# Keeping the split query weights of an expert layer in DRAM for the second choice of experts, with a sixth buffer for gathered rows

## The chip, the core and the metric

The kernel runs on one core of one Trainium2 chip. A core has five engines that run side by side and meet only at semaphores: PE (TensorE, the matmuls; PEld is its weight load), DVE (VectorE), ACT (ScalarE), POOL (GpSimd, which also issues the gathers) and SP (SyncE, which here only issues transfers). Each engine works through its own instructions in order. Sixteen DMA engines move data between DRAM and the on-chip memory. The metric is the device time of one execution in microseconds.

## What is computed

One encoder layer on 1024 tokens of width 1024: a norm, a combined projection, attention beside a retention branch, an output projection, and then a product-key expert layer on `xn = rmsnorm(x)`, which takes most of the time:

```
def peer_ffn(xn, w_query, sub_keys, expert_down, expert_up):
    def one_block(xb):                                  # 128 tokens
        q = (xb @ w_query).reshape(tb, 8, 2, 128)       # 8 heads, 2 halves
        s = einsum('thpd,hpnd->thpn', q, sub_keys)      # 128 keys each
        top_s, top_i = lax.top_k(s, 16)
        cand_s = top_s[:, :, 0, :, None] + top_s[:, :, 1, None, :]
        cand_i = top_i[:, :, 0, :, None] * 128 + top_i[:, :, 1, None, :]
        best_s, pos = lax.top_k(cand_s, 16)             # 128 experts a token
        eid = take_along_axis(cand_i, pos)
        gate = softmax(best_s)
        u = expert_down[eid]; act = gelu(einsum('thkd,td->thk', u, xb))
        v = expert_up[eid];   return einsum('thk,thkd->td', gate * act, v)
```

## The kernel before

**Two ways through the experts.** Tokens stand in tiles of 128. Five tiles (set B) pass through all 16384 experts as dense matmuls, with a gate matrix that is zero where an expert was not chosen. Three tiles (set A) gather only the chosen rows, one row per token and transfer. Both ways run at the same time in the last 1900 us: PE does the dense part, POOL issues gathers, and DVE consumes the gathered rows.

**Float32 by parts.** A matmul operand `w` is split into `wh`, a rounded copy (F32R), and `wl = w - wh`, and `mm3` (lines 72 to 75) makes a product of three matmuls. Each split costs a copy on ACT and a subtraction on DVE or POOL.

**The choice of experts** (`experts`, line 706) goes through 16 half heads `hp`. For each, `query` makes the projected query from the tokens and the weights of that half head (24 matmuls for two tiles), ACT and DVE split it, six matmuls per two tiles make the scores, and DVE picks the top 16 (`top16`) and combines the halves of a head (`choose`). It runs twice. The **early choice** (line 866) serves the five tiles of B and the first tile of A, has the weights in three buffers (`wb` = 3) and stands between the attention and the gate matrix. The **late choice** (line 962, inside `later`) serves the other two tiles of A. It is a generator of which `gathers` (line 1013) takes a step about once for each of the 128 groups of experts, so it lies inside the dense part. It has one weight buffer (`wb` = 1). In both, `weights` (line 642) loads `wqr`, 128 x 1152 floats or 576 KB, by SP, copies it to `wqh` on ACT and subtracts `wql` on POOL:

```
        def weights(pool, hp):
            wr = pool.tile([P, 9, P], F32, name="wqr")
            nc.sync.dma_start(wr, ap["wq"][hp])
            ...
            S.activation(wh, wr, AF.Copy)
            G.tensor_tensor(wl, wr, wh.bitcast(F32), op=ALU.subtract)
```

In the late choice the weights of `hp + 1` are asked for right after the scores of `hp` are issued, and the query of `hp + 1` is one step of the generator later.

**The dense part** goes through groups `a` of 128 experts. `down(a)` makes `pa` (48 matmuls on PE, lines 73 to 75), `up` makes `po` (30 matmuls per group, in five accumulators). After every second group DVE adds the five `po` to `acc` (line 1094), and the first `po` matmul of the next round waits for that addition. Per group SP loads `ur` (line 1034), `vr` twice (1079) and the gate `gt` (1043); ACT and DVE split them.

**The gathers** (`gather_tiles`, line 969): `rows` issues one indirect transfer of 512 KB on POOL into a buffer of the ring `rows` (line 977, `ROWS` = 5 buffers); a DVE instruction (line 988 for `peer_u`, 997 for `peer_v`) consumes it and frees the buffer. Six gathers belong to one group of the dense part. After the late choice a second ring of six (`rows2`) takes every second gather.

A scheduler puts the instructions of the engines in order from the program; the pools decide which tile may share room.

Of the kernel before, what the change touches and what calls it, by code (L numbers as in the profile page):

```python
# [10 lines left out]
F32 = mybir.dt.float32  # L11
F32R = mybir.dt.float32r
# [9 lines left out]
P = 128  # L22
# [6 lines left out]
HP = 16  # L29
# [6 lines left out]
RATE = 6.0  # L36
EVERY = 6
EARLY = 1.03
ROWS = 5

FIRST = 5
BEFORE = (10, 34, 58, 82, 106)
# [12 lines left out]
def peer_layer(tc, ap, dbg=None):  # L55
    nc = tc.nc
    V, S, G, PE = nc.vector, nc.scalar, nc.gpsimd, nc.tensor
# [14 lines left out]
    def mm3(out, ah, al, bh, bl, first, last):  # L72
        PE.matmul(out, ah, bh, start=first, stop=False)  # L73
        PE.matmul(out, ah, bl, start=False, stop=False)  # L74
        PE.matmul(out, al, bh, start=False, stop=last)  # L75

    with ExitStack() as top:
        const = top.enter_context(tc.tile_pool(name="const", bufs=1))
        dram = top.enter_context(tc.tile_pool(name="dram", bufs=1, space=DRAM))
# [41 lines left out]
        with ExitStack() as es:  # L121
# [212 lines left out]
            for gi, (half, nm) in enumerate(order):  # L334
# [4 lines left out]
                for c2 in range(DC // 2):  # L339
# [4 lines left out]
                    wh = pw.tile([P, 2, 512], F32R, name="wh", bufs=4)  # L344
                    wl = pw.tile([P, 2, 512], F32R, name="wl", bufs=4)
# [267 lines left out]
        w = (nB + 1) // 2 * P  # L613
# [4 lines left out]
        def query(pool, ps, segs, wh, wl, tag, aside):  # L618
            n = sum(e - b for seg in segs for _, b, e in seg)
            qh = pool.tile([P, n], F32R, name="pqh")  # L620
            ql = pool.tile([P, n], F32R, name="pql")
            at = 0
            for seg in segs:
                w = sum(e - b for _, b, e in seg)
                pq = ps.tile([P, w], F32, name=tag[0], bufs=tag[1])
                o = 0
                for nm, b, e in seg:
                    for c in range(DC):
                        mm3(pq[:, o:o + e - b], wh[:, c], wl[:, c], nT[nm][0][:, c, b:e], nT[nm][1][:, c, b:e],
                            c == 0, c == DC - 1)  # L630
                    o += e - b
                if aside:
                    q = pool.tile([P, w], F32, name="pqr")
                    S.activation(q, pq, AF.Copy)
                    split_q.append(S.activation(qh[:, at:at + w], pq, AF.Copy).ins)
                    G.tensor_tensor(ql[:, at:at + w], q, qh[:, at:at + w].bitcast(F32), op=ALU.subtract)
                else:
                    split(qh[:, at:at + w], ql[:, at:at + w], pq)
                at += w
            return qh, ql  # L640

        def weights(pool, hp):
            wr = pool.tile([P, 9, P], F32, name="wqr")
            nc.sync.dma_start(wr, ap["wq"][hp])
            wh = pool.tile([P, 9, P], F32R, name="wqh")
            wl = pool.tile([P, 9, P], F32R, name="wql")
            S.activation(wh, wr, AF.Copy)
            G.tensor_tensor(wl, wr, wh.bitcast(F32), op=ALU.subtract)
            return wh, wl

        pw0 = p0.enter_context(tc.tile_pool(name="wq0", bufs=1, side="right"))
        with ExitStack() as es:
# [26 lines left out]
            for u, (nm, i, t) in enumerate(todo):  # L679
# [4 lines left out]
                if u == 1:  # L684
                    first = weights(pw0, 0)
                if last is not None:
                    turned(ps, *last, "otp")
                    if last[0] == "A0":
                        first = first, query(pn, ps, SEGS, *first, ("pq", 1), False)
# [16 lines left out]
        def experts(sel, n, segs, pq_, pw, ps, wb, tags, bufs, first=None):  # L706
# [5 lines left out]
            def top16(vals, idxs, s, n, nm):  # L712
                V.max(vals[:, 0:8], s)
                V.max_index(idxs[:, 0:8], vals[:, 0:8], s)
                s2 = pw.tile([P, n], F32, name="s2" + nm)
                V.match_replace(s2, vals[:, 0:8], s, -3.4e38)
                V.max(vals[:, 8:16], s2)
                return V.max_index(idxs[:, 8:16], vals[:, 8:16], s2).ins
# [64 lines left out]
            def q_of(w):  # L783
                return query(pw, ps, segs, *w, (tags[0], bufs[0]), wb > 1)

            ws = {hp: weights(pq_[hp % wb], hp) for hp in range(first is not None, wb)}
            if first is not None:
                ws[0], cur = first
            else:
# [2 lines left out]
            for hp in range(HP):  # L792
                if hp % 2 == 0:
                    tv = pw.tile([P, n, 2, TOPK], F32, name="tv")
                    ti = pw.tile([P, n, 2, TOPK], U32, name="ti")
                (qh, ql), (wh, wl) = cur, ws[hp]
                more = hp + 1 < HP
                if wb > 1 and more and hp > 1:
                    cur = q_of(ws[hp + 1])
                yield  # L800
                sc = ps.tile([P, n, P], F32, name=tags[1], bufs=bufs[1])
                for t in range(n):
                    s = slice(t * P, t * P + P)
                    mm3(sc[:, t], qh[:, s], ql[:, s], wh[:, 8], wl[:, 8], True, True)
                if wb > 1 and more and hp < 2:
                    cur = q_of(ws[hp + 1])
                if hp + wb < HP:
                    ws[hp + wb] = weights(pq_[hp % wb], hp + wb)
                for t in range(n):
                    top = top16(tv[:, t, hp % 2], ti[:, t, hp % 2], sc[:, t], P, "s")  # L810
                    if t == 0:
                        first_top = top
                if hp % 2:
                    if wb > 1:
                        with tc.issue_after(first_top):
                            for _ in summing:
                                pass
                    else:
                        for _ in summing:
                            pass  # L820
                    waiting = hp // 2, pairs(tv), ti
                elif waiting:
                    summing = choose(*waiting)
                    next(summing)
                    waiting = None
                if wb == 1 and more:
                    yield
                    cur = q_of(ws[hp + 1])
# [33 lines left out]
        with ExitStack() as es:  # L862
            pq_ = {k: es.enter_context(tc.tile_pool(name=f"swq{k}", bufs=1)) for k in (1, 2, 0)}
# [84 lines left out]
        def later(ps):  # L948

            rest = SETS["A"][1:]  # L950
            with tc.tile_pool(name="se", bufs=1, side="right") as pe:
                n = len(rest)
                if n:
                    nT["A"] = [pe.tile([P, DC, n * P], F32R, name=n_) for n_ in ("nThA", "nTlA")]
                    for i, t in enumerate(rest):
                        xn = gp.tile([P, D], F32, name="rows", bufs=ROWS)
                        nc.sync.dma_start(xn, xn_dr[t])
# [11 lines left out]
        def gather_tiles(other):  # L969
            count = [0]  # L970

            def rows(table, idx):
# [3 lines left out]
                else:  # L976
                    u = gp.tile([P, D], F32, name="rows", bufs=ROWS)
                G.indirect_dma_start(out=u, out_offset=None, in_=table,  # L978
# [24 lines left out]
        with ExitStack() as es:  # L1003
# [108 lines left out]
            with tc.tile_pool(name="pro", bufs=1, side="right") as pp:  # L1112
                first = [pp.tile([P, DC * P], F32, name=f"first{a}") for a in range(FIRST)]
# [95 lines left out]
```

## Time and profile before

| What | us |
| --- | --- |
| median of three runs | 3129.86 (3127.61 to 3130.92) |
| the profiled execution, its own time | 3130.9 |
| its span, first to last instruction | 3129.1 |
| early choice, about | 630 to 890 |
| gate matrix, about | 890 to 1165 |
| dense part with the late choice in it, about | 1230 to 1930 |
| dense part without it, about | 1930 to 3087 |

The times of stages count from the span's start. Of the span PE is busy 91%, DVE 83%, POOL 55%, ACT 34%. These shares are means over stages with different limits, so the reading goes by stages.

### The profile page before, as it was taken

What the parts mean: (1) busy time and instruction counts of PE and PEld (TensorE: products, weight loads), DVE (VectorE), ACT (ScalarE), POOL (GpSimd) and SP (SyncE); (2) the same over time, 40 slices, a digit from 0 to 9 for tenths busy, and PEclk for the clock granted to TensorE, in tenths of its full rate; (3) what the DMA queues carried; (4) which work ended last, traced back from release to release, by engine and by line L of the source; (5) the groups of instructions that cost most, each with busy time, mean ns of one, the idle gap of its engine ahead of it and who ended that gap; (6) DMA issues with size and microseconds to landing.
All of it is one profiled execution on the core that took longest, in us unless ns stands there. A gap on an engine that the chain in (4) does not pass through costs nothing.

```text
span 3129.1 us, 44717 instructions
## 1 busy us (share of the span) xinstructions
PE 2850.7 (91%) x15999; PEld 2528.5 (81%) x15999; DVE 2589.1 (83%) x4867; ACT 1071.8 (34%) x1750; POOL 1706.6 (55%) x1319
## 2 busy tenths in 40 slices
PE   8999798898978847998899898999999999999998
PEld 6888577798977637887788787898999889998997
DVE  5465587579999946898998888888999988889997
ACT  4444466422247732222223222222222222222222
POOL 3422455346559944666556556565555465655551
PEclk9999899999999978999899999999999999999999
DMA  4334955331006688877777879999999899999994
GB/s 160 110 122 134 197 115 108 123 127 37 23 18 172 176 254 308 304 275 260 280 267 249 279 273 352 330 325 325 341 328 326 298 348 326 328 331 337 330 325 169
DMA packets 327919, 742.54 MB, mean 237 GB/s; under 512 B 25872, under 2 KB 133008, under 8 KB 327696
## 3 DMA queue, kind: packets, MB, share of 16 engines
q0 software_dynamic: 123520, 419.48, 39.2%
q1 hardware_dynamic: 201584, 315.28, 30.7%
q10 hardware_dynamic: 2592, 4.93, 0.5%
q8 instruction: 126, 2.06, 0.3%
q14 instruction: 97, 0.79, 0.1%
HBM read 669.26 MB, written 70.32 MB: 236 GB/s over the span
## 4 chain that ended last, share of the span: by engine, by line
PE 27%; DVE 15%; issue 14%; POOL 8%; DMA 5%; ACT 1%; SPq 1%; POOLq 0%; DVEq 0%; ACTq 0%
POOL rows L978 6%; PE po L73 5%; PE po L75 5%; PE po L74 5%; PE pa L73 4%; PE pa L74 4%; PE pa L75 4%; DVE gacc L997 4%; DVE rows L988 2%; DVE oh L910 2%; DMA rows<-peer_u,idx 2%; DMA ur<-ut 1%; POOL ao L917 1%; DVE acc L1094 1%; SPq L930 1%
## 5 line engine op out<-in xcount | busy, mean ns | idle before, releaser
L978 POOL DMA_INDIRECT rows<-peer_u,idx x384 | 525.8, 1369 | 401.6 <-DVE act L988 236.7
L978 POOL DMA_INDIRECT rows<-peer_v,idx x384 | 470.1, 1224 | 401.7 <-DVE gacc L997 338.4
L73 PE MATMUL pa<-nThB,uh 128*128 128x320 f32 x2048 | 639.0, 312 | 54.4 <-ACT uh L1050 39.4
L75 PE MATMUL pa<-nThB,ul 128*128 128x320 f32 x2048 | 636.0, 311 | 15.3 <-DVE ul L1051 15.3
L74 PE MATMUL pa<-nTlB,uh 128*128 128x320 f32 x2048 | 636.5, 311 | 0.0
L73 PE MATMUL po<-vh,hh 128*128 128x512 f32 x1280 | 516.0, 404 | 66.1 <-DVE acc L1094 65.9
L75 PE MATMUL po<-vh,hl 128*128 128x512 f32 x1280 | 509.6, 398 | 0.0
L74 PE MATMUL po<-vl,hh 128*128 128x512 f32 x1280 | 508.3, 397 | 0.7 <-DVE vl L1083 0.7
L997 DVE SCALAR_TENSOR_TENSOR gacc<-rows,act,gacc 128x1024 f32<-128x1024 f32 x384 | 502.9, 1310 | 5.5 <-DMA rows<-peer_v,idx 4.6
L988 DVE CUSTOM_DVE_ANT_0 rows<-rows,xng 128x1024 f32<-128x1024 f32 x384 | 467.0, 1246 | 44.8 <-DMA rows<-peer_u,idx 30.1
L73 PEld LDWEIGHTS pa<-nThB,uh 128*128 128x128 f32 x2048 | 389.9, 190 | 61.0 <-ACT uh L1050 39.6
L75 PEld LDWEIGHTS pa<-nThB,ul 128*128 128x128 f32 x2048 | 389.7, 190 | 16.6 <-DVE ul L1051 16.0
L74 PEld LDWEIGHTS pa<-nTlB,uh 128*128 128x128 f32 x2048 | 390.0, 190 | 4.4
L73 PEld LDWEIGHTS po<-vh,hh 128*128 128x128 f32 x1280 | 246.8, 193 | 124.5 <-DVE acc L1094 75.1
L1082 ACT ACTIVATE vh<-vr 128x512 fp32r<-128x512 f32 x256 | 160.2, 628 | 384.4 <-PE po L75 168.0
L75 PEld LDWEIGHTS po<-vh,hl 128*128 128x128 f32 x1280 | 246.2, 192 | 55.6
L74 PEld LDWEIGHTS po<-vl,hh 128*128 128x128 f32 x1280 | 246.7, 193 | 49.1 <-DVE vl L1083 1.5
L1050 ACT ACTIVATE uh<-ur 128x1024 fp32r<-128x1024 f32 x118 | 125.2, 1061 | 371.1 <-PE pa L74 199.1
L1051 DVE TENSOR_TENSOR ul<-ur,uh 128x1024 fp32r<-128x1024 f32 x118 | 145.7, 1234 | 102.6 <-ACT uh L1050 67.5
L917 POOL TENSOR_TENSOR ao<-oh,gT 128x512 f32<-128x512 bf16 x145 | 206.9, 1462 | 22.3 <-DVE oh L910 22.3
L923 PE MATMUL pg<-ao,bo 128*128 128x128 f32 x1280 | 181.5, 289 | 41.0 <-POOL ao L917 32.3
L858 ACT ACTIVATE hf<-pa 128x320 f32<-128x320 f32 x246 | 105.7, 430 | 328.4 <-PE pa L75 300.3
(344 smaller groups left out, 5481.3 us busy)
## 6 DMA issues: line engine op xcount, KB each, us to landing
vr<-peer_v SPq DMA_DIRECT2D x256, 256.0 KB
ur<-ut SPq DMA_DIRECT2D x123, 512.0 KB
g_dr<-stg SPq DMA_DIRECT2D x40, 1024.0 KB
gt<-g_dr SPq DMA_DIRECT2D x123, 320.0 KB
wr<-w_in SPq DMA_DIRECT2D x48, 512.0 KB
wqr<-wq SPq DMA_DIRECT2D x32, 576.0 KB
kt<-dk_dr POOLq DMA_DIRECT2D x16, 512.0 KB
xr<-xT SPq DMA_DIRECT2D x24, 256.0 KB
```

The lines of the kernel that those rows point to most:

```text
L73: PE.matmul(out, ah, bh, start=first, stop=False)
L74: PE.matmul(out, ah, bl, start=False, stop=False)
L75: PE.matmul(out, al, bh, start=False, stop=last)
L858: S.activation(hf[:, cs], pa, AF.Gelu)
L917: G.tensor_tensor(ao, oh[0], bc(gT[:, q:q + 4, None], [P, 4, P]), op=ALU.mult)
L923: PE.matmul(pg[:, j], bo[:, j], ao[:, j], start=True, stop=True)
L978: G.indirect_dma_start(out=u, out_offset=None, in_=table, in_offset=bass.IndirectOffsetOnAxis(ap=idx, axis=0))
L988: V.tensor_tensor_reduce(out=u, in0=u, in1=xn, scale=1.0, scalar=0.0, op0=ALU.mult, op1=ALU.add, accum_out=act[:, k:k + 1])
L997: V.scalar_tensor_tensor(o, v, act[:, k:k + 1], o, op0=ALU.mult, op1=ALU.add)
L1050: S.activation(uh, ur, AF.Copy)
L1051: V.tensor_tensor(ul, ur, uh.bitcast(F32), op=ALU.subtract)
L1082: S.activation(vh, vr, AF.Copy)
```

## The change

`weights` writes both parts of what it has split to a new DRAM tensor `wq_dr`, two stores of 576 KB on SP for each half head. The early choice goes through all 16 half heads, so all of them are written there (half head 0 by the call in the projection stage, line 685). The late choice calls `weights` with `made` true: no load of the raw weights, no copy on ACT, no subtraction on POOL; instead two loads of 576 KB, issued by POOL, straight into `wqh` and `wql`. Without `wqr` the late choice's pool is 4608 bytes a partition smaller, and `ROWS` goes from 5 to 6, which takes 4096.

```
-ROWS = 5
+ROWS = 6
...
-        def weights(pool, hp):
+
+        wq_dr = dram.tile([HP, 2, P, 9, P], F32, name="wq_dr")
+
+        def weights(pool, hp, made=False):
+            if made:
+                wp = [pool.tile([P, 9, P], F32R, name=n_) for n_ in ("wqh", "wql")]
+                for k in range(2):
+                    G.dma_start(wp[k], wq_dr[hp, k])
+                return wp
             wr = pool.tile([P, 9, P], F32, name="wqr")
             nc.sync.dma_start(wr, ap["wq"][hp])
...
             G.tensor_tensor(wl, wr, wh.bitcast(F32), op=ALU.subtract)
+            for k, w in enumerate((wh, wl)):
+                nc.sync.dma_start(wq_dr[hp, k], w.bitcast(F32))
             return wh, wl
...
-            ws = {hp: weights(pq_[hp % wb], hp) for hp in range(first is not None, wb)}
+            ws = {hp: weights(pq_[hp % wb], hp, wb == 1) for hp in range(first is not None, wb)}
...
-                    ws[hp + wb] = weights(pq_[hp % wb], hp + wb)
+                    ws[hp + wb] = weights(pq_[hp % wb], hp + wb, wb == 1)
```

Lines behind `weights` stand ten lines lower in the changed kernel (978 becomes 988, for instance).

POOL in the late choice, where it gathers rows of `peer_v`; before:

```order
L648 TENSOR_TENSOR wql<-wqr,wqh 128x1152
L978 DMA rows<-peer_v,idx 128x1024 x12
L648 TENSOR_TENSOR wql<-wqr,wqh 128x1152
L978 DMA rows<-peer_v,idx 128x1024 x13
L648 TENSOR_TENSOR wql<-wqr,wqh 128x1152
```

and now, at the same place:

```order
L649 DMA wqh<-wq_dr 128x1152
L649 DMA wql<-wq_dr 128x1152
L988 DMA rows<-peer_v,idx 128x1024 x13
L649 DMA wqh<-wq_dr 128x1152
L649 DMA wql<-wq_dr 128x1152
L988 DMA rows<-peer_v,idx 128x1024 x13
L649 DMA wqh<-wq_dr 128x1152
L649 DMA wql<-wq_dr 128x1152
```

Each subtraction has given its place between the gathers to two issues of transfers.

SP at the start of the late choice, where it loads for the dense part; before:

```order
L1034 DMA ur<-ut 128x1024
L1079 DMA vr<-peer_v 128x512
L644 DMA wqr<-wq 128x1152
L1034 DMA ur<-ut 128x1024
L1079 DMA vr<-peer_v 128x512 x2
L644 DMA wqr<-wq 128x1152
L1034 DMA ur<-ut 128x1024
```

and now:

```order
L1044 DMA ur<-ut 128x1024
L1089 DMA vr<-peer_v 128x512
L1044 DMA ur<-ut 128x1024
L1089 DMA vr<-peer_v 128x512 x2
L1044 DMA ur<-ut 128x1024
```

The loads of raw weights are gone from between those of the dense part.

SP in the middle of the early choice; before, six loads of raw weights in a row:

```order
L846 DMA ur<-ut 128x1024 x2
L644 DMA wqr<-wq 128x1152 x6
L879 DMA hf_dr<-hf 128x640
```

and now, of the same stretch, its beginning:

```order
L856 DMA ur<-ut 128x1024 x2
L658 DMA wq_dr<-wqh 128x1152
L658 DMA wq_dr<-wql 128x1152
L652 DMA wqr<-wq 128x1152
L658 DMA wq_dr<-wqh 128x1152
L658 DMA wq_dr<-wql 128x1152
L652 DMA wqr<-wq 128x1152
```

Two stores stand ahead of each load of raw weights.

## Rows read from the trace of the kernel before

**Rows 1.** Busy time by stage; columns: stretch, length, engines' busy us, clock, DMA share, GB/s.

```profile
630.00:890.00 260.00, 235.03 (x1657) 230.31 (x1655) 234.37 (x1308) 60.46 (x105) 145.73 (x95) 0.95 0.16 56
1230.00:1930.00 700.00, 630.12 (x3522) 569.60 (x3520) 625.83 (x1232) 194.86 (x298) 412.81 (x308) 0.95 0.80 277
1930.00:3087.00 1157.00, 1142.74 (x6328) 1035.17 (x6329) 1036.09 (x1380) 306.48 (x493) 644.27 (x498) 0.99 0.92 327
```

**Rows 2.** Waits, 1230 to 1930, PE's; columns: total us, times, longest us.

```profile
PE po L73 <- DVE acc L1094: 46.5, 16, 8.7
PE e L73 <- DVE cs L728: 7.1, 1, 7.1
PE e L73 <- DVE pql L67: 6.2, 1, 6.2
```

**Rows 3.** Waits, 1930 to 3087, PE's.

```profile
PE po L73 <- DVE acc L1094: 19.2, 10, 6.4
```

**Rows 4.** Timeline around one subtraction: start us, us, engine, line, names, [idle before].

```profile
1608.36 1.28 DVE L997 SCALAR_TENSOR_TENSOR gacc<-rows,act,gacc 128x1024 f32<-128x1024 f32 x1
...
1608.95 0.28 PE L75 MATMUL e<-wqh,pql 128*128 128x128 f32 x1
...
1610.86 3.09 POOL L648 TENSOR_TENSOR wql<-wqr,wqh 128x1152 fp32r<-128x1152 f32 x1
...
1611.55 3.48 DVE L997 SCALAR_TENSOR_TENSOR gacc<-rows,act,gacc 128x1024 f32<-128x1024 f32 x1
...
1618.34 0.67 DVE L1094 TENSOR_TENSOR acc<-po,acc 128x512 f32<-128x512 f32 x1
...
1619.06 0.50 PE L73 MATMUL po<-vh,hh 128*128 128x512 f32 x1 [2.05 <-DVE acc L1094]
```

**Rows 5.** Groups by line, 1230 to 1930: count, busy us, mean ns, idle before.

```profile
L997 DVE SCALAR_TENSOR_TENSOR gacc<-rows,act,gacc 128x1024 f32<-128x1024 f32 x128 | 175.6, 1372 | 4.9 <-DMA rows<-peer_v,idx 4.6
L988 DVE CUSTOM_DVE_ANT_0 rows<-rows,xng 128x1024 f32<-128x1024 f32 x115 | 147.8, 1306 | 21.4 <-DMA rows<-peer_u,idx 20.7 <-issue 0.6
...
L648 POOL TENSOR_TENSOR wql<-wqr,wqh 128x1152 fp32r<-128x1152 f32 x16 | 46.8, 2925 | 22.6 <-ACT wqh L647 22.2 <-issue 0.3
```

**Rows 6.** The same view, 1930 to 3087.

```profile
L997 DVE SCALAR_TENSOR_TENSOR gacc<-rows,act,gacc 128x1024 f32<-128x1024 f32 x251 | 320.9, 1279 | 0.7
L988 DVE CUSTOM_DVE_ANT_0 rows<-rows,xng 128x1024 f32<-128x1024 f32 x250 | 296.3, 1219 | 3.9 <-DMA rows<-peer_u,idx 3.9
```

**Rows 7.** Busy time, as rows 1, in two short stretches behind waits of PE.

```profile
1618.90:1623.00 4.10, 3.93 (x16) 2.92 (x17) 4.10 (x9) 1.07 (x2) 0.53 (x1) 1.00 0.72 259
1465.40:1469.00 3.60, 3.52 (x9) 2.79 (x10) 3.02 (x6) 0.10 (x1) 1.17 (x2) 0.55 0.93 311
```

**Rows 8.** Timeline of PE, the wait ahead of the second of these stretches.

```profile
1465.48 0.79 PE L73 MATMUL po<-vh,hh 128*128 128x512 f32 x1 [8.70 <-DVE acc L1094]
```

**Rows 9.** Waits, 1230 to 1930, DVE's.

```profile
DVE rows L988 <- DMA rows<-peer_u,idx: 20.7, 10, 5.3
DVE ul L1051 <- ACT uh L1050: 18.2, 7, 4.3
```

**Rows 10.** Waits of SP's queue, 1230 to 1930.

```profile
SPq L644 <- POOL wql L648: 72.1, 15, 11.7
```

**Rows 11.** Plain loads that POOL issues, in the attention: ns shortest/median/longest.

```profile
L111 POOL DMA_DIRECT2D kt<-dk_dr x16: 600/630/860, 313.1 to 482.7; - x16
```

**Rows 12.** Timeline, one gather and the DVE instruction that waits for it.

```profile
1855.21 0.98 POOL L978 DMA_INDIRECT rows<-peer_v,idx  x1 [4.94 <-DVE acc L1094]
...
1862.03 1.28 DVE L997 SCALAR_TENSOR_TENSOR gacc<-rows,act,gacc 128x1024 f32<-128x1024 f32 x1 [4.63 <-DMA rows<-peer_v,idx]
```

**Rows 13.** Timeline of PE, first matmuls of two queries.

```profile
1625.65 0.28 PE L73 MATMUL e<-nThA,wqh 128*128 128x256 f32 x1
...
1650.77 0.36 PE L73 MATMUL e<-nThA,wqh 128*128 128x256 f32 x1 [0.50 <-DVE eq L762]
```

**Rows 14.** Timeline of PE, last score matmul ahead of the second of them.

```profile
1642.91 0.28 PE L75 MATMUL e<-wqh,pql 128*128 128x128 f32 x1
```

**Rows 15.** Waits, 1230 to 1930, POOL's longest before a gather.

```profile
POOL rows L978 <- DVE gacc L997: 104.2, 68, 6.9
```

**Rows 16.** Waits in the early choice, 630 to 890, of PE and of SP's queue.

```profile
PE pq L75 <- POOL wql L648: 11.6, 4, 4.8
...
SPq L644 <- POOL wql L648: 87.6, 11, 20.0
```

## The prediction, made before the changed kernel ran

> **What bounds the kernel now.** I read the stages first, then who waits in the one that the change touches, then single instructions there. The table of stages [rows 1] sets two long stretches of the same dense work side by side. From 1930 to 3087 PE is busy 1142.74 of 1157 us at a mean granted clock of 0.99: PE is the bound. From 1230 to 1930, where the late choice runs in it, PE is busy 630.12 of 700 us at a mean clock of 0.95: it stands idle for 70 us and loses some 5% of 700, 35 us, to stretches at the lower of its two levels (1.2 instead of 2.4 GHz). So this stretch has at most about 105 us to give, and the other one its idle 14.
>
> Who makes PE wait there? DVE, nearly always: 46.5 us in 16 waits for the addition of line 1094, and two single waits of 7.1 and 6.2 for other DVE work [rows 2]. In the longer stretch without the late choice the same wait is 19.2 us [rows 3]. DVE is busy 625.83 of 700 us, 0.894, and its share is 0.896 from 1930 to 3087 and 0.901 in the early choice [rows 1]. So the late choice is bound by DVE as it really runs, with its short waits, and PE is let go late.
>
> The timeline shows why DVE is late [rows 4]. The instruction of line 997 takes 1.28 us at 1608.36. At 1610.86 POOL begins the subtraction `wql`, 3.09 us long; the same DVE instruction, begun at 1611.55 beside it, takes 3.48 us, 2.20 more. The addition for PE, behind it in DVE's order, starts only at 1618.34, and PE has stood for 2.05 us when it goes on at 1619.06. One subtraction has cost PE nearly what it cost DVE.
>
> **What the change removes in the late choice.** The 16 subtractions, 46.8 us of POOL with a mean of 2925 ns [rows 5], go. What they cost DVE is bounded twice. From above: 16 times 2.20 is 35 us. From below, by the two commonest DVE instructions alone: line 997 has a mean of 1372 ns here and 1279 without the late choice, 128 times 93 ns or 11.9 us; line 988 has 1306 against 1219, 115 times 87 ns or 10.0 us [rows 5, 6]; together 22 us. Fewer than the 16 subtractions can hit these two, so I take a value nearer to the upper end, 32 us. As DVE sets the pace of the stretch, and work on it is fixed per group, I count it in full: **-32 us**.
>
> By the Trainium skill (SBUF — State Buffer, Who interferes with whom) a DVE instruction with two inputs from the memory and a GpSimd instruction that reads it exclude each other for a whole instruction. Taken by the length of a subtraction, this would make the term 16 times 2.925, 46.8 us instead of 32. The row above has 2.20 of 3.09, since the DVE instruction had its own turn to wait for only in part, and the row decides.
>
> The second gain is PE's clock. Behind the wait of 2.05 us the granted clock stays at 1.00, and behind one of 8.70 us it is 0.55 on the mean over the next 3.6 us [rows 4, 7, 8]. With some 2 us off each of 16 waits, many of them fall to the length that left the clock alone. Of the 35 us between nothing and most may come back; but PE is ahead of DVE most of the time here, so a faster PE mainly waits longer. I take **-10** (0 to -25).
>
> The third is on the queues. SP stands 72.1 us in 15 waits with a load of raw weights at the head of its queue until POOL has subtracted [rows 10], and the loads of `ur` and `vr` stand behind it; the order shows these loads with nothing between them now. DVE waits 18.2 us for copies of `ur` and 20.7 us for gathered rows [rows 9]. The sixth buffer and the freed POOL and SP can return part of these 39 us, while nothing shortens the transfers themselves, and there are more bytes. I take **-5** (0 to -20). From 1930 on the sixth buffer can only touch the idle 14 us, most of it in the changes from one tile to the next: **-2** (0 to -6). ACT's 16 copies cover no end and count as nothing; ACT is busy 195 of 700 us [rows 1].
>
> **What it adds.** Each half head now has two transfers of 576 KB in place of one, by POOL. A plain load of 512 KB costs POOL 0.63 us [rows 11], so a pair costs some 1.3 instead of 2.9: POOL gains. The pair can be issued only when the scores of the half head before are done, as the buffer is single, and the next query stands behind it on PE. The slack: scores done at 1609.23 and query at 1625.65, 16.4 us [rows 4, 13]; in the shortest case 1643.19 and 1650.77, 7.6 us [rows 13, 14]. The need: a gather of 512 KB is used 6.8 us after POOL began it [rows 12]; the second of a pair begins later by 0.6, and 576 KB more at 277 GB/s [rows 1] is 2.1 us, so about 10 us as an estimate. On top POOL may stand with a gather ahead of the pair, up to 6.9 us [rows 15]: 10 to 17. So most queries find their weights, and a few wait some us. From below this is zero; from above 15 waits of 2 to 3 us, with clock, some 50. I take **+6**: three waits of 2.
>
> Against the issue by POOL speaks the Trainium skill (SBUF — State Buffer, A bandwidth-pool intuition that's wrong (but worth ruling out)): a transfer issued by GpSimd can take some 3100 ns instead of 620 while DVE holds the ports. By its figures 32 issues would cost POOL 79 us more than I count and each pair would come 5 us later, which is the slower rival below. No row here has a plain load of POOL beside gathered rows.
>
> The added bytes are small against the stretch: 16 times 0.59 MB net in 700 us is 13 GB/s on 277, at a DMA share of 0.80; the next stretch runs at 327 and 0.92 [rows 1].
>
> In the early choice SP gets 32 stores. DMA is at 0.16 there [rows 1], so the bytes hide. The stores wait for ACT and POOL, and behind them stands the next load of raw weights; but that load waited for the same subtraction before, 87.6 us in 11 waits [rows 16], and had a buffer in hand. PE waits 11.6 us for `wql` in that stage [rows 16], which could double. In the projection two loads of the residual stand behind a store, a us or two each. At the start of the dense part a sixth gather, 512 KB, goes ahead of the first tile's activations, 1.6 us at 327 GB/s. Together **+3** (-3 to +15).
>
> **Sum.** -32 - 10 - 5 - 2 + 6 + 3 = -40, from the profiled execution's 3130.9 to 3090.9; that execution lies 1.0 above the median, so **3090** against 3129.86. A check that uses none of these terms but the first: DVE's work in the stretch is 626 - 32 = 594 us; at the share of 0.894 at which it runs in three stages it takes 664 us, 36 less than 700. After 1930 PE is the bound with its own fixed work, so what the late choice returns reaches the end.
>
> **The rivals.**
> *The gain is larger* (14%): DVE's waits shrink too, and DVE comes to 0.94 of the stretch: 594 / 0.94 = 632, 68 less, with +9 of new costs and -2 later: about 3069. For it speaks that PE has 105 us to give; against it that no stage shows DVE above 0.90.
> *The gain goes into other waits* (16%): DVE, 32 us earlier, meets gathered rows and `ur` that have not landed, since their transfers are what they were, with more bytes on the same DMA engines. For it speak the 39 us of such waits now. If two thirds of the 32 go there and the clock returns nothing, 11 are left, and with +9, -5 and -2 the time is about 3121 (3114 to 3128).
> *Slower, by late weights* (10%): each of 15 pairs lands 6 us after PE reaches its query, as POOL is held at gathers and the pair is slow behind them. PE in order stands 15 times 6, 90 us, and pays for each wait about half of the 3.6 us behind it in clock, 27 more: 117. DVE catches up in these waits, so the present 105 us of idle and clock go, and with +3 from the early choice the time is about 3145. It decides from a wait of about 5 us per pair: 15 times 6.8 is then what is lost now. Against it stands the slack of 16.4 us.
> *The forecast* has 60%, 3072 to 3108.
>
> **The range.** Below 3058 I leave some 6%, above 3120 some 13%: 3058 to 3120. A measurement of this kernel can tell about 0.2%, 6.3 us, from no change. Faster by more than that: the forecast, the larger gain, and half of the third case, 0.82; the same 0.08; slower 0.10.
>
> **What would show it.** In the stretch of the late choice, which should be about 660 us long instead of 700: line 997's counterpart back near 1280 ns on the mean, and none of 3.4 us; PE's waits for line 1094's counterpart about 20 instead of 46.5 us; the mean clock at 0.96 to 0.97; SP without a wait for POOL; PE's waits at the first matmul of a query under 10 us in total. The early choice should be as long as before within 5 us. Wrong would be: waits for the two loads above 30 us; DVE's waits for rows above 40 us; a longer early choice; or a stretch as long as before with shorter DVE instructions, which would mean that DVE did not set its pace.

## The result and the profile after

The changed kernel takes 3088.0 us (median of four runs, 3082.46 to 3094.69) against 3128.74 for the kernel before, beside which it ran: a ratio of 0.9874, 95% interval 0.9849 to 0.9899, or 40.7 us less. The forecast was 3090, within 3058 to 3120. The profiled execution is the fastest of the four, 3082.46 us with a span of 3080.7, and that of the kernel before took 3130.9; so the rows below show a gain of 48.4 us instead of 40.7.

Busy time by stage; columns as in [rows 1]. The windows begin 7 us earlier than in [rows 1], since this execution is some 7 us ahead of the other before the first instruction that the change touches (the first query matmul of the early choice begins at 622.9 instead of 629.8), and the second ends where the late choice's work ends now:

```profile
623.00:883.00 260.00, 236.81 (x1658) 232.16 (x1656) 233.99 (x1296) 60.49 (x105) 144.32 (x95) 0.94 0.34 123
1223.00:1878.00 655.00, 616.92 (x3542) 560.16 (x3541) 600.36 (x1239) 180.45 (x285) 390.92 (x324) 0.98 0.87 311
1878.00:3038.00 1160.00, 1144.54 (x6330) 1036.08 (x6331) 1035.52 (x1378) 306.07 (x493) 640.02 (x498) 0.99 0.92 326
```

The stretch with the late choice is 655 us long where it was 700. DVE's work in it went from 625.83 to 600.36 us, and the clock from 0.95 to 0.98. The other two stages are as they were.

Groups by line in that stretch, changed kernel; columns as in [rows 5]:

```profile
L1007 DVE SCALAR_TENSOR_TENSOR gacc<-rows,act,gacc 128x1024 f32<-128x1024 f32 x128 | 166.3, 1299 | 5.5 <-DMA rows<-peer_v,idx 5.3
L998 DVE CUSTOM_DVE_ANT_0 rows<-rows,xng 128x1024 f32<-128x1024 f32 x115 | 140.5, 1243 | 10.4 <-DMA rows<-peer_u,idx 10.1
...
L649 POOL DMA_DIRECT2D wql<-wq_dr x16 | 9.6, 600 | 2.8 <-PE e L75 2.7
L649 POOL DMA_DIRECT2D wqh<-wq_dr x16 | 9.5, 592 | 0.0
```

The two commonest DVE instructions fell from 1372 to 1299 ns and from 1306 to 1243 [rows 5]; the longest of line 1007 is 2.07 us, where line 997 had one of 3.64. They did not fall quite to the 1279 and 1219 of the last stretch [rows 6], where POOL does almost nothing but gather: in the late choice it still multiplies and adds small tiles. With the multiplications on DVE (e9, below) the means are 1290 and 1234 ns, against 1299 and 1239 of the changed kernel in the same window (1230 to 1930); that the additions make up the rest is not shown. The 46.8 us of subtractions have become 19.1 us of issues.

PE's waits in the same stretch (total us, times, longest):

```profile
PE po L73 <- DVE acc L1104: 19.6, 13, 4.7
PE e L73 <- DMA wqh<-wq_dr: 7.0, 2, 4.7
PE e L73 <- DVE act L998: 1.9, 1, 1.9
PE e L73 <- DVE ti L728: 1.5, 1, 1.5
PE pa L75 <- DVE ul L1061: 1.1, 1, 1.1
PE e L75 <- DMA wql<-wq_dr: 0.8, 1, 0.8
```

The wait for the addition was 46.5 us [rows 2]. New are three waits for the two loads, 7.8 us in all. The longest, in PE's timeline:

```profile
1713.80 0.36 PE L73 MATMUL e<-nThA,wqh 128*128 128x256 f32 x1 [4.69 <-DMA wqh<-wq_dr]
```

DVE's waits for rows and for copies of `ur`, against the 20.7 and 18.2 of [rows 9]:

```profile
DVE ul L1061 <- ACT uh L1060: 19.4, 7, 5.7
DVE rows L998 <- DMA rows<-peer_u,idx: 10.1, 7, 5.0
```

SP's queue, 1230 to 1930, the head of the list. No wait for POOL is in it; the 72.1 us of [rows 10] have not vanished but turned into longer waits of the dense part's own loads for their buffers:

```profile
SPq L1053 <- DVE hl L1077: 211.8, 32, 15.6
SPq L1089 <- DVE vl L1093: 167.2, 71, 7.7
```

And the early choice (623 to 883), PE's longest wait and SP's two for the new stores, against [rows 16]:

```profile
PE pq L75 <- POOL wql L656: 11.8, 5, 3.3
```

```profile
SPq L658 <- POOL wql L656: 75.5, 14, 9.5
SPq L658 <- ACT wqh L655: 50.7, 8, 11.8
```

SP stands longer for the split weights, 126.2 us against 87.6; PE does not: from the first query matmul to the last score the early choice takes 239.3 us, before 239.6.

### The profile page after: what moved, and what is told of

Same layout as the page of the kernel before. It is cut to its first block, busy times and chain, and to the rows that moved or that the text cites. A ratio compares the mean times of both kernels' runs of the same rounds, so it can differ in the third digit from the quotient of the medians.

```text
span 3080.7 us, 44740 instructions
## 1 busy us (share of the span) xinstructions
PE 2830.5 (92%) x15999; PEld 2512.8 (82%) x15999; DVE 2556.9 (83%) x4867; ACT 1055.1 (34%) x1734; POOL 1678.9 (54%) x1335
## 4 chain that ended last, share of the span: by engine, by line
PE 19%; issue 17%; DVE 16%; POOL 10%; DMA 7%; ACT 2%; SPq 1%; POOLq 0%; DVEq 0%; ACTq 0%
POOL rows L988 8%; DVE rows L998 3%; PE po L73 3%; PE po L75 3%; DVE gacc L1007 3%; PE po L74 3%; PE pa L73 3%; PE pa L74 3%; PE pa L75 3%; DVE oh L920 2%; DMA ur<-ut 2%; DMA rows<-peer_u,idx 1%; DVE acc L1104 1%; DMA vr<-peer_v 1%; POOL ao L927 1%
## 5 line engine op out<-in xcount | busy, mean ns | idle before, releaser
L1007 DVE SCALAR_TENSOR_TENSOR gacc<-rows,act,gacc 128x1024 f32<-128x1024 f32 x384 | 493.3, 1285 | 6.2 <-DMA rows<-peer_v,idx 5.3
L998 DVE CUSTOM_DVE_ANT_0 rows<-rows,xng 128x1024 f32<-128x1024 f32 x384 | 459.3, 1226 | 34.9 <-DMA rows<-peer_u,idx 20.5
L75 PEld LDWEIGHTS pa<-nThB,ul 128*128 128x128 f32 x2048 | 387.8, 189 | 15.8 <-DVE ul L1061 15.4
```

Of the source, the lines that this page charges most:

```text
L998: V.tensor_tensor_reduce(out=u, in0=u, in1=xn, scale=1.0, scalar=0.0, op0=ALU.mult, op1=ALU.add, accum_out=act[:, k:k + 1])
L1007: V.scalar_tensor_tensor(o, v, act[:, k:k + 1], o, op0=ALU.mult, op1=ALU.add)
```

## One stretch of the same work in every kernel

All kernels below are compared in one stretch: from the first to the 41st product `gt` (line 1070 of the changed kernel) on DVE. It holds 40 groups of the dense part and the whole late choice but for its first load of weights, so nearly the same work in each. Each row is one row of the view of busy time, between the starts of these two instructions; DVE's idle time is the length less its busy time. All but the last column come from a single profiled execution each, whose own time can lie some us off the median: 3100.54 us for e1, 3082.46 and 3092.08 for the changed kernel.

| Kernel | length us | DVE busy | DVE idle | PE busy | PE clock | time, median us |
| --- | --- | --- | --- | --- | --- | --- |
| before | 700.4 | 630.56 | 69.8 | 629.81 | 0.94 | 3128.74 |
| changed | 650.4 | 601.41 | 49.0 | 612.24 | 0.98 | 3088.0 |
| changed, again (e8) | 660.9 | 603.31 | 57.6 | 617.90 | 0.97 | 3090.63 |
| five row buffers (e1) | 671.8 | 603.27 | 68.5 | 626.14 | 0.95 | 3097.62 |
| e1 and holds, early (e2) | 705.1 | 633.83 | 71.3 | 631.90 | 0.93 | 3133.39 |
| e1 and holds, spread (e11) | 706.4 | 634.59 | 71.8 | 630.49 | 0.94 | 3134.96 |
| e1 and fills on POOL (e6) | 668.5 | 603.15 | 65.4 | 620.60 | 0.96 | 3098.96 |
| before, DVE subtracts (e3) | 674.0 | 620.29 | 53.7 | 622.67 | 0.96 | 3102.39 |
| before and stores (e4) | 697.4 | 630.34 | 67.1 | 629.81 | 0.94 | 3124.36 |
| before, SP free (e7) | 695.4 | 631.64 | 63.8 | 629.48 | 0.95 | 3125.11 |
| changed, loads by SP (e5) | 658.0 | 600.85 | 57.2 | 616.43 | 0.97 | 3089.9 |
| changed, `eq` on DVE (e9) | 654.4 | 603.75 | 50.7 | 615.83 | 0.97 | 3082.6 |
| changed, seven rows (e10) | 653.8 | 601.64 | 52.2 | 617.32 | 0.97 | 3081.74 |
| e9 and split pair (e12) | 656.1 | 603.13 | 53.0 | 615.47 | 0.98 | 3089.33 |

Read the DVE columns. With five row buffers DVE is idle for 64 to 72 us, except in e3 (53.7), and the length follows its busy time. With six or seven the idle time is 49 to 58. The medians of the last column lie beside runs of the kernel before of 3127.6 to 3129.2.

## The experiments

The theories. **A**, that of the prediction: the subtraction on POOL held DVE, DVE sets the pace of the late choice, and so its lengthened instructions were the time. **B**: the chain load, copy, subtraction counted, with SP and POOL standing in it. **C**: it was the sixth buffer.

### The sixth buffer taken back

```
-ROWS = 6
+ROWS = 5
```

> The changed kernel with ROWS = 5 again, so only the sixth buffer is taken back. Theory A (the subtraction on POOL held DVE, and DVE sets the pace of the late choice): the sixth buffer gives few us, 3089 to 3097, ratio to before 0.987 to 0.990; DVE's waits for gathered rows in the stretch of the late choice go up by under 8 us from 15.4. Rival C (the sixth buffer brought the gain, since DVE's idle time in the stretch fell by some 19 us and its waits for rows by 10): 3110 or more, ratio 0.994 and above, and DVE's waits for rows back at 25 us or more.

Measured: 3097.62 us (3093.04 to 3100.54), ratio 0.9895, interval 0.9881 to 0.9909: 0.6 us above the range of theory A, 12 below that of C. DVE's waits in its stretch:

```profile
DVE rows L998 <- DMA rows<-peer_u,idx: 19.1, 11, 4.6
DVE gacc L1007 <- DMA rows<-peer_v,idx: 8.4, 4, 5.3
```

Three quarters of the gain, 31 us of 41, need no sixth buffer; in the table they are DVE's work (27.3 us less) with the idle time as before. The waits for rows, 27.5 us, are above the 15.4 of the changed kernel, by more than theory A had allowed.

> The changed kernel as it is, beside the runs of this call. Both theories: 3083 to 3093. Against e1_five_rows (3097.6) this gives the sixth buffer alone: theory A had 3 to 8 us for it; from e1 it is now 5 to 14.

Measured: 3090.63 us (3078.04 to 3092.36), ratio 0.9871, interval 0.9845 to 0.9897. So the sixth buffer is worth 7 to 10 us by the medians. The intervals of e1 and of the changed kernel overlap, so its size is not certain; that it is there also shows in DVE's idle time in the table, 11 to 20 us less than in e1.

### The hold put back, alone

```
 for k in range(2):
     G.dma_start(wp[k], wq_dr[hp, k])
+scr = pool.tile([P, 9 * P], F32, name="scr")
+still = [nT["B"][0]...[:, b:b + 9 * P] for b in (0, 9 * P)]
+G.tensor_tensor(scr, still[0], still[1], op=ALU.subtract)
```

> As e1, and in each of the 16 late half heads POOL also subtracts two pieces of a tile that never changes, 128 x 1152 floats, into a scratch tile which nobody reads; it waits for nothing. This puts back POOL's reading beside DVE and nothing else of what was removed. Theory A: DVE's instructions in the stretch get longer again by 25 to 32 us in all (mean of the peer_v accumulation about 1370 ns, single ones of 3 us and more), and the time is 25 to 35 us above e1. Rival B (what counted was the chain load, copy on ACT, subtraction, and SP and POOL standing in it): none of this chain comes back, so under 8 us above e1.

Measured: 3133.39 us (3126.18 to 3140.87), ratio 1.0013, interval 1.0003 to 1.0023: 35.8 above e1 (33.2 between the two profiled executions), all of the gain gone and a little more. The view of the added instruction's tile, and the groups by line in 1230 to 1930, of e1 and then of this kernel:

```profile
L652 POOL TENSOR_TENSOR scr<-nThB x16: 2642/2836/3537, 1238.8 to 1320.1; 128x1152 f32<-128x1152 f32 x16
```

```profile
L1007 DVE SCALAR_TENSOR_TENSOR gacc<-rows,act,gacc 128x1024 f32<-128x1024 f32 x128 | 166.4, 1300 | 8.7 <-DMA rows<-peer_v,idx 8.4
L998 DVE CUSTOM_DVE_ANT_0 rows<-rows,xng 128x1024 f32<-128x1024 f32 x127 | 155.1, 1243 | 19.1 <-DMA rows<-peer_u,idx 19.1
L1104 DVE TENSOR_TENSOR acc<-po,acc 128x512 f32<-128x512 f32 x105 | 66.0, 679 | 0.0
L1070 DVE TENSOR_TENSOR gt<-gt,hf 128x640 f32<-128x640 f32 x41 | 35.0, 854 | 6.6 <-ACT hf L868 6.5
```

```profile
L1010 DVE SCALAR_TENSOR_TENSOR gacc<-rows,act,gacc 128x1024 f32<-128x1024 f32 x128 | 166.6, 1301 | 9.6 <-DMA rows<-peer_v,idx 9.3
L1001 DVE CUSTOM_DVE_ANT_0 rows<-rows,xng 128x1024 f32<-128x1024 f32 x111 | 148.8, 1360 | 20.6 <-DMA rows<-peer_u,idx 20.6
L1107 DVE TENSOR_TENSOR acc<-po,acc 128x512 f32<-128x512 f32 x95 | 59.9, 680 | 0.0
L1073 DVE TENSOR_TENSOR gt<-gt,hf 128x640 f32<-128x640 f32 x39 | 40.7, 1043 | 4.9 <-ACT hf L871 4.8
L652 POOL TENSOR_TENSOR scr<-nThB 128x1152 f32<-128x1152 f32 x16 | 47.5, 2972 | 0.9
```

Since they depend on nothing, the scheduler put all 16 subtractions into the first 81 us. That makes the case sharper than it was meant: of the two commonest DVE instructions only that for `peer_u` runs there, and only its mean rises (1360 ns, in e1 1243); line 1010 runs later and is as short as in e1. Not all of DVE's work is held: the product `gt`, with both inputs in the on-chip memory SBUF, rises from 854 to 1043 ns, and the addition to `acc`, one of whose inputs (`po`) comes from PE's accumulators, stays at 680. Busy time of e1 and of this kernel in the first ten groups and in the other thirty (columns as in [rows 1]); e1:

```profile
1242.50:1404.40 161.90, 154.22 (x883) 140.23 (x882) 144.53 (x326) 41.71 (x68) 95.82 (x76) 0.97 0.91 317
1404.40:1914.30 509.90, 471.92 (x2619) 425.61 (x2619) 458.74 (x918) 133.56 (x210) 290.24 (x249) 0.95 0.85 303
```

and with the subtractions:

```profile
1245.20:1438.50 193.30, 159.40 (x885) 144.22 (x886) 175.41 (x327) 41.26 (x68) 137.08 (x90) 0.90 0.75 260
1438.50:1950.30 511.80, 472.50 (x2613) 426.36 (x2612) 458.42 (x919) 133.64 (x210) 294.43 (x249) 0.95 0.85 302
```

Where the subtractions are (14 of them in this window), the same DVE instructions take 30.9 us longer and the time is 31.4 us longer; where they are not, both are as in e1. DVE's lengthening became time one for one, and no other part of the old chain was there. The clock fell from 0.97 to 0.90 in the same ten groups, and no time beyond DVE's went with it.

```
+pair = [w.bitcast(F32)... for w in wp]
+G.tensor_tensor(scr, *pair, op=ALU.subtract)
```

> As e2_hold_back (ROWS = 5, a subtraction of 128 x 1152 on POOL into a scratch tile for each late half head), but the subtraction reads the pair of tiles that was just loaded. In e2 it depended on nothing, and 13 of the 16 stood in the first ten groups of the dense part; here they lie spread over the late choice as in the kernel before, and POOL waits for the landing of the pair as it waited for ACT before. Theory A: DVE's instructions longer by 25 to 34 us in all, spread over the stretch, and 25 to 36 us above e1, 3123 to 3134. Rival D (e2's loss came from the place, all holds at the start and the first query 20 us later; spread out, they vanish in DVE's 67 us of idle time): under 12 us above e1, below 3110.

Measured: 3134.96 us (3125.0 to 3142.47), ratio 1.0021, interval 1.0006 to 1.0037: 37.3 above e1, a little more than theory A had. The groups by line in 1230 to 1930:

```profile
L1010 DVE SCALAR_TENSOR_TENSOR gacc<-rows,act,gacc 128x1024 f32<-128x1024 f32 x128 | 173.1, 1352 | 18.3 <-DMA rows<-peer_v,idx 18.1
L1001 DVE CUSTOM_DVE_ANT_0 rows<-rows,xng 128x1024 f32<-128x1024 f32 x114 | 145.0, 1289 | 24.2 <-DMA rows<-peer_u,idx 23.8
L652 POOL TENSOR_TENSOR scr<-wqh,wql 128x1152 f32<-128x1152 f32 x16 | 49.3, 3083 | 46.5 <-DMA wql<-wq_dr 28.5 <-DMA wqh<-wq_dr 18.0
```

Spread over the late choice as in the kernel before, the holds cost the same. Both line means are up again, and rival D falls. Against the kernel before this one has what else the change does, with five buffers, holds of 49.3 instead of 46.8 us, and POOL's wait of 46.5 us for the pairs; it is 6 us slower (2 to 12 by the interval).

### The same engine busy without reading memory

```
+for _ in range(2):
+    G.memset(scr, 0.0)
```

> As e1, and in each of the 16 late half heads POOL fills a scratch tile of 128 x 1152 floats twice with zeros (nobody reads it): POOL is busy for a like time but reads no memory. Theory A: DVE's instructions are not lengthened, as a fill has no input to take from the memory, and the time is 0 to 6 us above e1; POOL's gathers come some us later, and slack takes that. Rival B, in the form that POOL's time delayed the gathers: as far above e1 as e2 is, 15 to 35 us, with DVE's waits for rows longer.

Measured: 3098.96 us (3089.28 to 3105.42), ratio 0.9898, interval 0.9882 to 0.9914: 1.3 above e1. Groups by line in 1230 to 1930, and busy time in the first ten groups, as above for e1 and e2:

```profile
L1001 DVE CUSTOM_DVE_ANT_0 rows<-rows,xng 128x1024 f32<-128x1024 f32 x128 | 156.7, 1246 | 22.3 <-DMA rows<-peer_u,idx 22.3
L652 POOL MEMSET scr<- 128x1152 f32 x32 | 34.3, 1070 | 1.0
```

```profile
1242.40:1404.80 162.40, 153.78 (x888) 139.75 (x887) 144.94 (x326) 41.49 (x68) 125.26 (x107) 0.98 0.90 317
```

The fills, 34.3 us of POOL, lie in the same early place as the subtractions of e2 (the last begins at 1366). In the ten groups POOL is busy 29.4 us more than in e1 and DVE only 0.4. POOL's time is not what counted; an instruction on POOL that reads the memory is. The fills are shorter than the 47.5 us of e2, so the two are not of one size, but nothing of the kind that e2 shows is there at all.

### The subtraction on DVE

```
-G.tensor_tensor(wl, wr, wh.bitcast(F32), op=ALU.subtract)
+(en or G).tensor_tensor(wl, wr, wh.bitcast(F32), op=ALU.subtract)   # late choice: DVE
```

> The kernel before with the 16 late subtractions on DVE instead of POOL; all else as before (ROWS = 5, raw weights loaded by SP, copy on ACT). DVE then pays each subtraction itself: 1.37 us by the 1.223 us of the subtraction of 128 x 1024, 16 of them 22 us, and is not held by POOL any more, 25 to 32 us. Theory A: 3 to 10 us faster than before, 3119 to 3126, ratio 0.996 to 0.999. Rival B (POOL's time of 47 us and its waits for ACT, 22 us, counted): 20 us or more faster, ratio below 0.9935.

Measured: 3102.39 us (3093.38 to 3116.03), ratio 0.9917, interval 0.9897 to 0.9936, 26 us faster than before. Groups by line:

```profile
L997 DVE SCALAR_TENSOR_TENSOR gacc<-rows,act,gacc 128x1024 f32<-128x1024 f32 x128 | 166.4, 1300 | 11.1 <-DMA rows<-peer_v,idx 11.0
L988 DVE CUSTOM_DVE_ANT_0 rows<-rows,xng 128x1024 f32<-128x1024 f32 x127 | 157.9, 1262 | 13.4 <-DMA rows<-peer_u,idx 13.3
L648 DVE TENSOR_TENSOR wql<-wqr,wqh 128x1152 fp32r<-128x1152 f32 x16 | 22.1, 1384 | 5.0 <-ACT wqh L647 5.0
```

The sizes of work were as expected: 22.1 us of DVE's own, no hold, DVE's busy time down by 10.3 us net (table). The time was not: the stretch is 26.4 us shorter, as DVE's idle time fell by 16 as well. That is the number which rival B had given, and theory A missed it, but B has no support in e2, e6 and e7. DVE's waits in the common stretch tell where the 16 us lie: those for ACT's copies of `ur`, `vr` and `gt` (`ul`, `vl`, `hl`) fell from 28.7 to 12.6 us, those for POOL's `eq` from 6.9 to 1.6, and 3.8 for `wqh` came new; those for rows stayed (25.3 and 24.3). Why they fell, no run shows.

### The chain's other parts, one by one

```
 # before, and in the early choice:
+for k, w in enumerate((wh, wl)):
+    nc.sync.dma_start(wq_dr[hp, k], w.bitcast(F32))
```

> The kernel before plus the 32 stores of the split weights in the early choice, which nobody reads; the late choice as before. The price of the stores alone. Theory A: between 3 us faster and 6 us slower than before, 3126 to 3135, the early choice (first query matmul to last score) within 2 us of 239.6. Rival G (the stores hold the loads of raw weights behind them, and the changed kernel hides that only in its gain): 8 to 15 us slower.

Measured: 3124.36 us (3119.9 to 3128.04), ratio 0.9991, interval 0.9982 to 1.0001. The early choice takes 240.5 us. The stores cost nothing that shows.

```
-nc.sync.dma_start(wr, ap["wq"][hp])
+q.dma_start(wr, ap["wq"][hp])        # late choice: POOL's queue
```

> The kernel before with the 15 late loads of raw weights on POOL's queue instead of SP's; copy on ACT and subtraction on POOL as before. SP no longer stands 72 us behind them, and nothing else of the change is there. Theory A: SP's relief is worth little by itself, 0 to 6 us faster than before, 3123 to 3129, with DVE's instructions as long as before. Rival B in its form for SP (its blocked queue delayed the dense part's loads): 12 us or more faster, 3117 or less.

Measured: 3125.11 us (3118.19 to 3127.79), ratio 0.9992, interval 0.9982 to 1.0001. SP no longer stands for POOL; the time is 2.5 us less, by the interval between nothing and 5.6. The 72.1 us of SP's wait were hardly a loss, and rival B falls for SP. (POOL has the issues of these loads in return; what they cost is in the 2.5 us.)

```
-G.dma_start(wp[k], wq_dr[hp, k])
+nc.sync.dma_start(wp[k].bitcast(F32), wq_dr[hp, k])
```

> The changed kernel with the 32 late loads of the pair on SP's queue instead of POOL's. SP's queue stands up to 15.6 us at a time for other tiles (178 us in 28 waits for the split of the gate), so theory A expects the pair to be issued later: PE's waits for the two tiles 15 to 40 us in place of 7.8, and 0 to 20 us slower than the changed kernel, 3088 to 3108. Rival E (what POOL's 19 us of issues cost the gathers is worth more than the later pair): up to 8 us faster, 3080 to 3087, with DVE's waits for rows shorter.

Measured: 3089.9 us (3085.3 to 3094.78), ratio 0.9884, interval 0.9859 to 0.9908, the same as the changed kernel beside it. PE's waits for the pair are 9.6 us (10.3 in e8), not 15 to 40: the expectation that SP would bring the pair late was wrong, and so was rival E. Which queue loads the pair made no difference that can be told.

### Three tries for a faster version

```
-(V if last and not a else G).tensor_tensor(eq, ...
+(V if wb == 1 or (last and not a) else G).tensor_tensor(eq, ...
```

> The changed kernel with the 15 multiplications of eq (128 x 512, 1.36 us each) of the late choice on DVE instead of POOL. They read memory on POOL too: with the shorter POOL instructions around them they lengthen DVE's by 10.4 us in all in the profile of the changed kernel, and DVE waits 4.4 us for them. On DVE one takes 0.69 us (a single row of the profile), 15 of them 10.4. Theory A (hold and wait against work): between 6 us faster and 4 us slower, no change that can be told. Rival F (as in e3_dve_sub, work on DVE fills idle time of its own, and the queue of POOL is worth something besides the hold): 6 to 15 us faster.

Measured: 3082.6 us (3081.03 to 3091.35), ratio 0.9864, interval 0.984 to 0.9888; 8.0 us under e8 beside it by the medians and 5.4 under the first runs of the changed kernel. By the number that is the range of rival F, but the intervals overlap, in the table its stretch of 654.4 us lies between the two of the changed kernel, and its profiled execution is 5 us ahead of e8's already at the first query matmul of the early choice, which the edit does not touch. So it is no change that can be told, and neither A nor F is decided. By the table DVE's work is as it was (603.75 and 603.31): 10.3 us more of its own for about as much less of hold.

```
+ws[hp + 2] = weights(pq_[0], hp + 2, QUERY)   # blocks 0 to 7, after the query of hp + 1
+keys = weights(pq_[0], hp + 1, KEYS)          # block 8, after the scores of hp
```

> The kernel of e9_eq_on_dve with the late pair cut in two: the part that the query needs (8 of 9 blocks) is loaded as soon as the query before has been made, one step of the generator earlier than now, and only the ninth block, which the scores need, after the scores. Same room. If PE's waits for the loads (8 to 13 us in the late choice of the three runs so far) are worth their length, they go to under 3 us and the time is 4 to 10 us below e9 (3082.6), 3073 to 3079; if DVE sets the pace through them, as theory A has it, PE's gain becomes waiting for DVE and the time is within 4 us of e9, 3079 to 3086; the 32 further issues cost POOL 19 us, which slack takes.

Measured: 3089.33 us (3085.39 to 3092.18), ratio 0.988, interval 0.9865 to 0.9895: 6.7 above e9, outside both ranges, though the intervals overlap. PE's waits in e9's stretch and in this one's:

```profile
PE po L73 <- DVE acc L1104: 22.3, 12, 6.0
PE e L73 <- DMA wqh<-wq_dr: 12.7, 4, 6.5
```

```profile
PE po L73 <- DVE acc L1114: 25.4, 14, 7.1
PE po L73 <- DVE act L1008: 7.3, 1, 7.3
PE e L73 <- DVE s2s L727: 6.3, 1, 6.3
PE pa L75 <- DVE ul L1071: 1.5, 1, 1.5
```

The waits for the loads, 13.4 us with 0.7 for `wql`, are gone to the last, and PE waits for DVE instead: 40.5 us of waits in all, before 38.3. So no gain came of taking the waits for the late pairs away. That they were free is likely but not shown, since the 32 further issues on POOL may have cost what the waits had.

```
-ROWS = 6
+ROWS = 7
-... bufs=2 * GB - 1)     # hh, hl
+... bufs=2 * GB - 2)
```

> The changed kernel with a seventh row buffer; its room comes from hh and hl, which go from seven buffers to six. If the ring of rows is still a limit (the sixth gave about 7 us), 2 to 6 us faster than the changed kernel, 3084 to 3088, with DVE's waits for rows down from 15 to 18 us. If the transfers themselves are the limit, no gain; and if the seventh pair of hh and hl let PE run ahead of DVE, slower by 5 to 20 us, with new waits of ACT or DVE for PE.

Measured: 3081.74 us (3079.74 to 3082.3), ratio 0.9855, interval 0.984 to 0.9871. DVE's waits for rows are 13.1 us. It is the lowest median of all, 6 to 9 us under the two medians of the changed kernel; the intervals overlap, and in the table its stretch of 653.8 us lies between the two of the changed kernel. So it is a hint and no proof that a seventh buffer gives something more.

## Why the prediction was right, step by step

**What bounds the late choice.** Right, and now shown, though DVE's share was no sign of it: it is 0.896 also from 1930 on, where PE is the bound. e2 lengthens DVE's instructions alone, and the time follows one for one in just that place.

**The hold, -32 (22 to 35).** Right in kind and size. Without it DVE's work in the common stretch falls by 27.3 us (e1), where 15 of the subtractions lay; with it again it rises by 30.6 for the 14 that lie in the stretch in e2 and by 31.3 for 16 in e11. That is 1.8 to 2.2 us for each subtraction of some 3. The time follows with 36 to 37 us by the medians. The prediction's reading of a single timeline, 2.20 of 3.09 us [rows 4], was near. The Trainium skill's rule (SBUF — State Buffer, Who interferes with whom), by which the two exclude each other for a whole instruction, would by itself give 46.8. The 14 of e2, 41.6 us by their mean, lengthened DVE by 30.6, so this upper bound is not reached. In [rows 4] 2.40 us of the subtraction were left when the DVE instruction began, and it took 2.20 longer. Of the same section the other half, that a GpSimd instruction which only writes doesn't contend with one of DVE with two inputs, is borne out by e6: with 29.4 us more of POOL in the ten groups DVE is busy 144.94 us against 144.53.

**The clock, -10 (0 to -25).** This was the step that failed. The clock did rise, from 0.95 to 0.98 in the stretch, a little more than the forecast 0.96 to 0.97, and in the table PE's busy time fell by 17.6 us for the same work. But beside the hold it is no second gain. From before to e1 the stretch is 28.6 us shorter and DVE's work 27.3; from e1 to e2, in the first ten groups, the clock falls to 0.90 and the time rises by DVE's 30.9 and half a microsecond. PE ahead of DVE only waits, as the prediction itself said and then counted 10 all the same. Hold and clock together were put at -42; the runs have -36 to -37. Whether the clock has a share in what the sixth buffer gives (0.95 in e1, 0.97 and 0.98 with six) no run separates.

**SP free and the sixth buffer, -5 (0 to -20), and -2 later.** The parts were mixed up. SP's relief is worth nothing to 5.6 us (e7). The buffer is worth 7 to 10, more than the whole term. Later it gives nothing: from the 41st product to the last it is 1138.3 us before, 1142.6 and 1142.2 in the two profiles of the changed kernel, 1138.0 with five buffers.

**The late pairs, +6 (0 to 50).** The waits were forecast well, three of 2 us, and came as three of 4.7, 2.3 and 0.8. As a price they may have been too high: e12 takes them away and gains nothing. By e11, with POOL standing 46.5 us for the landing of the pairs on top, all of the change besides hold and buffer costs about 6 us; what of that is the pairs was not separated. POOL's issues took 592 to 600 ns beside DVE's work, where the Trainium skill's 3100 ns (SBUF — State Buffer, A bandwidth-pool intuition that's wrong (but worth ruling out)) would have made the rival true; the trace doesn't show such a starved issue. The same page reports it for a copy on DVE, and this stretch has two-input instructions there.

**The early choice and the stores, +3 (-3 to +15).** Too cautious: e4 gives -3 us, with an interval that touches none.

**The sum** came out at -40 against -40.7 in part by luck: 10 us for a clock that gave nothing beside the hold stood in for a hold and a buffer that were put some us too low and for costs that were put some us too high. By the runs it reads: hold -36 to -37, sixth buffer -7 to -10, the rest of the change about +6 (e11). The check that used only DVE's work at a fixed share, -36, was the soundest step: the share did stay in e1 (0.898 of the common stretch, 0.900 before), where the gain is 31.

**The signs.** The stretch was to be about 660 us long: 650 and 661. Line 1007 near 1280 ns: 1299, with none of 3.4 us. The wait for line 1104 about 20 us: 19.6. The clock 0.96 to 0.97: 0.98, and 0.97 in e8. SP without a wait for POOL: so. PE's waits at a query under 10 us: 10.4 at the first matmul, just missed. The early choice as long as before: so.

**The rivals.** That the gain goes into other waits is refuted by e1 (31 us with idle time unchanged), the late weights by the result (7.8 us of waits for the pairs, not 90), and so is the larger gain: DVE reached 0.92 of the common stretch, 0.91 in e8, not 0.94.

## What to carry to other kernels

Where DVE sets the pace, an instruction that reads on-chip memory on POOL isn't free help: here 16 of them, 2.97 us each, cost DVE some 2 us each, more than the 1.38 us for which DVE does the same subtraction itself. Moving it to DVE gave 26 us; storing the result, which is needed twice, and loading it again gave 31 with the same buffers, in spite of more bytes (the intervals of e3 and e1 overlap), and made room for one more buffer. Here DMA had room for that and the loads had slack. And in a stretch that one engine paces, count the gain on that engine once; the clock and the waits of the engine behind it are the same time seen again.

## What was not expected

Doing the subtraction on DVE gave 26 us of the 41 by naming another engine for one instruction, some 12 more than the hold less DVE's own work (36 less 22); DVE's waits for ACT's copies shrank, and why is open. SP's 72 us in the queue behind POOL were worth less than 6 us. And one row buffer more, at unchanged transfers, was worth more than that.
